# A hybrid attention/mLSTM layer: a tenth projection pair by seven products, the last gate multiplied in on chip, and the output projection's sums and loads held in order

## The chip, the cores and the metric

One core of a Trainium2 chip runs the whole layer in one launch. The metric is the device time in microseconds (us) of that core. The engines are TensorE (PE for its matmuls, PEld for its weight loads), VectorE (DVE), ScalarE (ACT), GpSimd (POOL) and SyncE (SP). DMAs are issued from two queues: SP's for most transfers, POOL's for the operands of the last stage. An engine takes its instructions in the order that was fixed when the program was built.

## The reference, cut to what matters

```python
hn = rmsnorm(x, norm_w)
proj = hn @ w_in            # q, k, v, g of 8 attention heads; qk, v, o, z, gates of 4 mLSTM heads
att = neighbourhood_attention(q, k, v, na_rpb) * silu(na_g)
h = rmsnorm(bidirectional_mlstm(silu(conv(qk)), mv, gates), head_norm_w)
mem = h * sigmoid(ml_o) * silu(ml_z)
y = rmsnorm(x + concat(att, mem) @ w_out)
```

x has 1280 tokens (1024 of a prompt and 256 of a sample) of 2048 channels in float32; concat(att, mem) has 2048 channels, 1024 of each.

## The kernel before, in words

Each float32 operand is split into a high part and a remainder (`split`, L163: ACT casts the high part, DVE subtracts it from the source), and a product is three matmuls: high by high, high by low, low by high.

**Input projection.** The output channels are taken in 128-wide columns numbered 0 to 55 (q from 0, k from 8, g from 16, qk from 24, o from 40, z from 48) and always in pairs: "pair 14" is columns 14 and 15, the k of heads 6 and 7. The first 768 tokens go first, by `pair_a` (L468). The other 512 come later, a pair in one of two ways:

- `proj_pair` (L650) multiplies directly: 4 weight pieces of 512 KB, 96 matmuls of 512 columns (L662; the trace calls them pc), 8 splits.
- `pair_s` (L1342) forms the four 256x256-blocked products from seven (Strassen's way): 7 pieces of 512 KB, 14 splits, 168 matmuls of 256 columns (L1379; their banks carry the pair's number, as S22b). Four of the seven weight operands are sums that `pair_a` of the same pair has formed already on POOL; for each pair in the list SECOND it also stores these, 16 DMAs of 128 KB (L525), into sD. `finish_s` of a pair runs between the products of the next one.

The nine pairs in SECOND go through `pair_s` one after the other (L1450). The rest go through `proj_pair` while attention runs: they are filler for TensorE. The program's order comes from a scheduler that plays the whole program on a modelled timeline; attention and mLSTM units have priority (`run`, L1304), and what is written after them fills the holes.

**Attention and mLSTM.** Head h of attention loads its q and k (2 MB, L844 and L845, into one buffer, nap{h}qk) when they have been projected and the buffer is free. The eight pairs of o and z columns are taken last of all (`late_gate`, L695, called at L1477 for 0, 2, 4, 6). For its two z columns it forms z_ = (tanh(o/2)+1) * (tanh(z/2)+1) * z, loads the mLSTM result of the same channels from mixT in DRAM (into th, named lt), multiplies with the head-norm weight w4, and stores it back into mixT (L705 to L707).

**Output projection.** With attention finished its pool is closed, and the pool mp takes its place. POOL then issues the 32 loads of the mixed operands (`mix_block`, L1490, tiles mb, 320 KB each): Ad and Ac are the mLSTM half for tokens 0 to 639 and 640 to 1279, Aa and Ae the attention half. The output has 2 halves of columns (p = 0, 1), each again by seven products (`product`, L1607), in the order 2, 5, 1, 6, 7, 4, 3 for p = 0 and 5, 1, 6, 7, 4, 3, 2 for p = 1. A product has 8 steps kk of 5 token tiles x 3 matmuls of 512 columns (L1613): 120 matmuls. `operands` (L1528) makes the operands of a step: weights straight from DRAM by `w_pure` (two steps in one 512 KB piece: wr_wp in one of the two buffers "wraw" that the input projection uses too, wp in the single buffer "wr2" of mp), or as a difference of blocks loaded by `w_block` (256 KB, wb, in one of six buffers "po", which also hold the outputs pco of `proj_pair` and lt), and for some products sums of mb tiles, all on DVE. T2 (T in the trace) is a running weight difference; its tiles, the residual tiles y (`y_init`, L1564) and fnb (the final norm's weight, L1652) lie where the projected x was, so their loads wait for the last late gate's matmuls on that x. Splits go into four buffers each for mo (mixed operand) and wo (weight).

In these names po2, or wr_wp_2_6, carries the product and the step: product 2, step 6.

Of the kernel before, what the change touches and what calls it, by code (L numbers as in the profile page):

```python
# [11 lines left out]
ALU = mybir.AluOpType  # L12
# [26 lines left out]
    GT0, QK0 + 8, GT0 + 2, QK0, KT0, GT0 + 4, KT0 + 2, GT0 + 6, KT0 + 4,  # L39
)  # L40
# [5 lines left out]
def kernel(  # L46
# [116 lines left out]
    def split(hi, lo, src, scale=None):  # L163
        if scale is None:
            S.copy(hi, src)  # L165
            V.tensor_tensor(lo, src, f(hi), op=ALU.subtract)  # L166
        else:
            S.mul(hi, src, scale)
            V.scalar_tensor_tensor(lo, src, scale, f(hi), op0=ALU.mult, op1=ALU.subtract)
# [525 lines left out]
    def late_gate(ch, X):  # L695
        os_ = proj_pair(OT0 + ch, X, True)
        for o_ in os_:
            S.activation(o_, o_, AF.Tanh, scale=0.5)
        for j, z_ in enumerate(proj_pair(ZT0 + ch, X, True)):
            k = 8 + ch + j  # L700
            th = po(f"lt{k}")[:, :GB]
            S.activation(th, z_, AF.Tanh, scale=0.5)
            V.scalar_tensor_tensor(z_, th, 1.0, z_, op0=ALU.add, op1=ALU.mult)
            V.scalar_tensor_tensor(z_, os_[j], 1.0, z_, op0=ALU.add, op1=ALU.mult)
            DM.dma_start(th, mixT[k][:, GA:])  # L705
            V.scalar_tensor_tensor(z_, th, w4_sb[:, k - 8 : k - 7], z_, op0=ALU.mult, op1=ALU.mult)
            DM.dma_start(mixT[k][:, GA:], z_)  # L707

# [768 lines left out]
    for ch in LATE:  # L1477
        late_gate(ch, X)
# [18 lines left out]
    Ac = [mix_block(1, 1, kk) for kk in range(8)]  # L1497
    Aa = [mix_block(0, 0, kk) for kk in range(8)]
# [5 lines left out]
    pair_of = {}  # L1504

    def w_block(kh, nb, kk, name):
        raw = po(f"wb_{name}")[:, :512]
        DM.dma_start(raw, w_o[nb, :, (8 * kh + kk) * 512 : (8 * kh + kk + 1) * 512])
        return raw

    def w_pure(kh, nb, kk, name):
        k = 8 * kh + kk
        if kk % 2 == 0:
            src = w_o[nb, :, k * 512 : (k + 2) * 512]
            pair_of["n"] = pair_of.get("n", -1) + 1
            if pair_of["n"] % 3 == 2:
                pair_of["w"] = mp.tile([P, 1024], F32, tag="wr2", name=f"wp_{name}")
                DM.dma_start(pair_of["w"], src)
            else:
                pair_of["w"] = w_piece(src, f"wp_{name}")  # L1520
        return pair_of["w"][:, (kk % 2) * 512 : (kk % 2 + 1) * 512]
# [82 lines left out]

    HOLD = 2

    def product(p, i, bk, first, each):  # L1607
        held = []
        tail = (p, i) == (1, 2)
# [9 lines left out]
        for kk in range(8):  # L1619
            nm = f"{p}_{i}_{kk}"  # L1620
            ms, wsrc = operands(p, i, kk)
# [13 lines left out]
            split(*w, wsrc)  # L1635
# [15 lines left out]
    for i in range(4):  # L1651
        DM.dma_start(fnb[i], fnw[i * 512 : (i + 1) * 512].partition_broadcast(P))  # L1652
    SUB = ALU.subtract
    for p in range(2):
# [27 lines left out]
        product(p, 1, ch, True, reads(ch, (0, ALU.add), done=0 if p == 0 else None))  # L1682
        y_init(p, 2)
# [96 lines left out]
```

## Time and profile before

| what | value |
|---|---|
| time of 3 runs | 2558.35, 2562.34 (median), 2562.83 us |
| the profiled execution's own time | 2565.18 us |
| its span, first to last instruction | 2563.3 us |
| granted TensorE clock, mean | 0.997 |
| PE busy, PEld busy | 2534.0 us (99%), 2368.6 us (92%) |
| DVE, ACT, POOL busy | 1972.6, 1345.0, 615.3 us |

Where the stages lie in the span, by the trace: the first projection to 1097 us, the nine pairs of SECOND from about 1173 to 1350 us, attention with its fillers to 2113 us, the rest of the late gates to 2160 us, the output projection to 2554 us. A row of the timeline has its start, its length, engine, line, operation, tiles and count, and in brackets the idle time before it and what ended that. "SPq" rows are DMA issues on SP's queue. In a row of the table by stretches, each engine's busy time is followed by its number of instructions; then come the granted clock, the busy share of the DMA engines and GB/s.

### The profile page before, as it was taken

The numbers are of one execution on the slowest core, as the hardware profiler recorded it, in microseconds if no ns is written. First come the engines' busy times: TensorE is split into PE (matmuls) and PEld (weight loads), VectorE is DVE, ScalarE is ACT, GpSimd is POOL, SyncE is SP. The second block draws the span as 40 slices with busy tenths as digits, with TensorE's granted clock in tenths as the row PEclk, the third lists the DMA queues.
The fourth block names the chain that finished last, engine by engine and source line by source line (L and its number), as shares of the span: only waits on it lengthen the run. The fifth ranks groups of instructions, "written<-read, shape, count | busy, mean of one in ns | idle before, by whom it ended". The sixth has DMA issues, their size and how long they took to land.

```text
span 2563.3 us, 44540 instructions
## 1 busy us (share of the span) xinstructions
PE 2534.0 (99%) x15054; PEld 2368.6 (92%) x15054; DVE 1972.6 (77%) x4029; ACT 1345.0 (52%) x3041; POOL 615.3 (24%) x909
## 2 busy tenths in 40 slices
PE   8999999999999999999999999999999999999998
PEld 8999999999999999999999999998988887788886
DVE  8769888888869798898875866765855665879695
ACT  8535545444444444465655666655745543344444
POOL 0535555444544444410001110100100104000001
PEclk9999999999999999999999999999999999999999
DMA  6546464536434342467768878877867849636237
GB/s 215 174 143 200 143 199 130 179 124 200 125 112 126 101 141 89 154 228 223 239 223 299 297 243 272 293 234 261 286 197 251 277 126 377 202 125 218 85 87 254
DMA packets 303483, 503.03 MB, mean 196 GB/s; under 512 B 48752, under 2 KB 191256, under 8 KB 303256
## 3 DMA queue, kind: packets, MB, share of 16 engines
q1 hardware_dynamic: 299096, 484.46, 58.9%
q0 software_dynamic: 4160, 15.73, 1.6%
q8 instruction: 119, 1.95, 0.3%
q14 instruction: 108, 0.88, 0.1%
HBM read 373.13 MB, written 126.95 MB: 195 GB/s over the span
## 4 chain that ended last, share of the span: by engine, by line
PE 92%; DMA 5%; DVE 2%; issue 1%; ACT 1%; SPq 0%; POOL 0%; ACTq 0%; POOLq 0%; DVEq 0%
PE pc L662 16%; PE po L1613 14%; PE pv L740 5%; PE fb L274 2%; PE A24b L274 1%; PE A12b L274 1%; PE A16b L274 1%; PE A44b L274 1%; PE A48b L274 1%; PE A52b L274 1%; PE A40b L274 1%; PE A20b L274 1%; PE A8b L274 1%; PE A50b L274 1%; PE A42b L274 1%; PE A22b L274 1%
## 5 line engine op out<-in xcount | busy, mean ns | idle before, releaser
L1613 PE MATMUL po<-wo,mo 128*128 128x512 f32 x1620 | 376.9, 393 | 3.7 <-ACT wo L165 2.8
L1613 PEld LDWEIGHTS po<-wo,mo 128*128 128x128 f32 x1620 | 303.6, 188 | 76.2 <-ACT wo L165 4.2
L166 DVE TENSOR_TENSOR ws<-wr,ws 128x512 fp32r<-128x512 f32 x152 | 104.3, 696 | 53.2 <-ACT ws L165 52.4
L165 ACT CAST ws<-wr 128x512 fp32r<-128x512 f32 x152 | 92.5, 617 | 70.1 <-PE pc L662 57.5
L165 ACT CAST mo<-mb 128x640 fp32r<-128x640 f32 x72 | 51.8, 726 | 92.5 <-PE po L1613 73.7
L116 POOL TENSOR_SCALAR rs<-rs 128x1 f32<-128x1 f32 x10 | 3.4, 341 | 351.2 <-DVE rs L1593 351.1
L166 DVE TENSOR_TENSOR mo<-mb,mo 128x640 fp32r<-128x640 f32 x72 | 59.1, 827 | 27.1 <-ACT mo L165 27.0
L1562 DVE TENSOR_TENSOR y<-y,po 128x512 f32<-128x512 f32 x90 | 58.5, 687 | 11.3 <-PE po L1613 11.0
L165 ACT CAST mo<-ms 128x640 fp32r<-128x640 f32 x40 | 28.9, 726 | 61.1 <-PE po L1613 32.1
L166 DVE TENSOR_TENSOR wsv<-wr_v,wsv 128x512 fp32r<-128x512 f32 x64 | 44.4, 700 | 14.2 <-ACT wsv L165 13.9
L165 ACT CAST wsv<-wr_v 128x512 fp32r<-128x512 f32 x64 | 39.0, 617 | 26.8 <-PE pv L740 15.5
L1576 ACT ACTIVATE jk<-y 128x512 f32<-128x512 f32 x40 | 25.2, 631 | 36.5 <-DVE y L1562 36.2
L413 DVE SCALAR_TENSOR_TENSOR pcv<-pco,cw_sb,pcv 128x516 f32<-128x516 f32 x48 | 36.7, 764 | 7.1 <-ACT pcv L407 7.0
L166 DVE TENSOR_TENSOR mo<-ms,mo 128x640 fp32r<-128x640 f32 x40 | 32.8, 823 | 7.6 <-ACT mo L165 7.6
L129 ACT ACTIVATE xq<-xq 128x1024 f32<-128x1024 f32 x20 | 21.2, 1061 | 31.7 <-DMA xq<-in_xtok_dram 29.2
L1081 POOL MEMSET mls_0v<- 128x2 f32 x4 | 0.4, 102 | 145.1 <-DVE S_dt.float L166 119.7
L274 PE MATMUL fb<-xg,fw 128*128 128x384 f32 x192 | 34.6, 334 | 0.0
L251 DVE TENSOR_TENSOR pco<-pc,rstdb 128x512 f32<-128x512 f32 x30 | 20.6, 687 | 17.8 <-PE pc L662 17.1
L274 PEld LDWEIGHTS fb<-xg,fw 128*128 128x128 f32 x192 | 33.4, 188 | 0.0
L778 DVE CUSTOM_DVE_ANT_0 nap_0st<-nap_0s,nap_0bt 128x384 f32<-128x384 f32 x32 | 17.7, 555 | 20.1 <-PE nap_0s L773 8.7
L1525 DVE TENSOR_TENSOR ms<-mb,mb 128x640 f32<-128x640 f32 x40 | 32.8, 823 | 0.0
L1492 POOL DMA_DIRECT2D mb<-mx x32 | 17.7, 554 | 58.8 <-DVE ws L166 24.8
(2655 smaller groups left out, 8512.4 us busy)
## 6 DMA issues: line engine op xcount, KB each, us to landing
wr<-in_w_in_dram SPq DMA_DIRECT2D x76, 512.0 KB, 4.7
wr_v<-in_w_in_dram SPq DMA_DIRECT2D x32, 512.0 KB, 5.0
wb<-in_w_o_dram SPq DMA_DIRECT2D x48, 256.0 KB, 3.0
xq<-in_xtok_dram SPq DMA_DIRECT2D x20, 512.0 KB, 4.2
mb<-mx POOLq DMA_DIRECT2D x32, 320.0 KB, 8.2
wr_wp<-in_w_o_dram SPq DMA_DIRECT2D x16, 512.0 KB, 4.0
vS<-vo SPq DMA_DIRECT2D x24, 256.0 KB, 5.1
nap_0bt<-in_rpb_tab_dram SPq DMA_DIRECT2D x32, 192.0 KB, 4.3
```

The lines of the kernel that those rows point to most:

```text
L129: S.activation(raw, raw, AF.Square, accum_out=ssq[g][:, t, q : q + 1])
L165: S.copy(hi, src)
L166: V.tensor_tensor(lo, src, f(hi), op=ALU.subtract)
L251: V.tensor_tensor(o, src, rb, op=ALU.mult)
L274: PE.matmul(o, w(a_), x(b_), start=first and m == 0, stop=last and m == 2)
L413: V.scalar_tensor_tensor(dst[:, a:n], src[:, a + j - pad : n + j - pad], cw_sb[:, ct, j : j + 1], dst[:, a:n], op0=ALU.mult, op1=ALU.add,)
L662: PE.matmul(pb[j], t[j][:, wi, c : c + P], xs[xi], start=first and m == 0, stop=last and m == 2,)
L740: PE.matmul(outs[tt], xs[:, tt * P : (tt + 1) * P], t[:, wi, q * w : (q + 1) * w], start=first and m == 0 and (gates or tt % 2 == 0), stop ...
L1525: V.tensor_tensor(t, x, y_, op=op)
L1562: V.tensor_tensor(Y[p, q, tt], Y[p, q, tt], bk, op=op)
L1576: S.activation(jk, Y[p, q, tt], AF.Square, accum_out=ss[t][:, c : c + 1])
L1613: PE.matmul(bk[tt], m[xi][:, tt * P : (tt + 1) * P], w[wi], start=first and kk == 0 and j == 0, stop=last and j == 2, skip_group_check=True,)
```

## The change

1. Pair 14 (KT0 + 6, the k of heads 6 and 7) joins SECOND: `pair_a` stores its four sums, `pair_s` takes it as the tenth, and it is no filler any more.
2. For the last late gate (ch = 6, channels 14 and 15) the load, multiplication and store through mixT are left out; z_ is kept, and multiplied into the last 512 tokens of the tiles Ac[6] and Ac[7] once these are loaded.
3. Loads: the first of every three `w_pure` pieces takes the buffer wr2, before it was the third. The residual tiles y of p = 0 other than q = 0 go to SP's queue instead of POOL's. The loads of y and fnb are traced inside a product, at step `when`, and queued on SP behind the last `w_block` load traced until then.
4. Sums: each DVE instruction that `operands` issues for step kk is placed behind the previous product's split of its step kk. This and the queueing in 3 fix a place in an engine's order; they add no wait.

```diff
 SECOND = (
     GT0, QK0 + 8, GT0 + 2, QK0, KT0, GT0 + 4, KT0 + 2, GT0 + 6, KT0 + 4,
+    KT0 + 6,
 )
...
     def late_gate(ch, X):
+        held = []
...
             V.scalar_tensor_tensor(z_, os_[j], 1.0, z_, op0=ALU.add, op1=ALU.mult)
+            held.append(z_)
+            if ch == LATE[-1]:
+                continue
             DM.dma_start(th, mixT[k][:, GA:])
...
+    for j, z_ in enumerate(last_gates):
+        k = LATE[-1] + j
+        t = Ac[k][:, GA - TH :]
+        V.scalar_tensor_tensor(t, t, w4_sb[:, k : k + 1], z_, op0=ALU.mult, op1=ALU.mult)
...
-            if pair_of["n"] % 3 == 2:
+            if pair_of["n"] % 3 == 0:
...
-            q_ = DM if p else G
+            q_ = DM if p or q else G
...
+    def scales(p):
+        for i in range(4 if p == 0 else 0):
+            DM.dma_start(fnb[i], fnw[i * 512 : (i + 1) * 512].partition_broadcast(P))
...
-            ms, wsrc = operands(p, i, kk)
+            if loads is not None and kk == when:
+                with tc.issue_after(last_load["ins"]) if kk else ExitStack():
+                    loads()
+            with tc.issue_after(done[kk]) if done else ExitStack():
+                ms, wsrc = operands(p, i, kk)
...
-            split(*w, wsrc)
+            now.append(split(*w, wsrc).ins)
...
+        done[:] = now
...
-        y_init(p, 1)
-        y_init(p, 3)
-        product(p, 5, bk, True, reads(bk, (1, ALU.add), (3, ALU.add)))
+        product(
+            p, 5, bk, True, reads(bk, (1, ALU.add), (3, ALU.add)),
+            lambda: (y_init(p, 1), y_init(p, 3)), 0 if p else 5,
+        )
...
-        product(p, 1, ch, True, reads(ch, (0, ALU.add), done=0 if p == 0 else None))
-        y_init(p, 2)
+        product(
+            p, 1, ch, True, reads(ch, (0, ALU.add), done=0 if p == 0 else None),
+            lambda: (scales(p), y_init(p, 2)), 3,
+        )
```

What moves, at three places. Up to the end of pair 6 TensorE's order is the same in both, but for the 168 matmuls of the tenth pair. First place: TensorE at the end of pair 6 (q of heads 6 and 7), the last direct pair ahead of the late gates, of before:

```order
L662 MATMUL pc6_1_19031<-x1_15h_13111,ws_6_31_19133 128x512 x2
L662 MATMUL pc6_1_19031<-x1_15l_13112,ws_6_31_19133 128x512
L662 MATMUL pc14_0_19184<-x1_0l_12804,ws_14_00_19188 128x512
L662 MATMUL pc14_0_19184<-x1_0h_12803,ws_14_00_19188 128x512 x2
L662 MATMUL pc14_0_19184<-x1_1l_12813,ws_14_00_19188 128x512
L662 MATMUL pc14_0_19184<-x1_1h_12812,ws_14_00_19188 128x512 x2
```

and of the changed kernel at the same place:

```order
L663 MATMUL pc6_1_19307<-x1_15h_13131,ws_6_31_19409 128x512 x2
L663 MATMUL pc6_1_19307<-x1_15l_13132,ws_6_31_19409 128x512
L663 MATMUL pc40_0_25388<-x1_0l_12824,ws_40_00_25392 128x512
L663 MATMUL pc40_0_25388<-x1_0h_12823,ws_40_00_25392 128x512 x2
L663 MATMUL pc40_0_25388<-x1_1l_12833,ws_40_00_25392 128x512
L663 MATMUL pc40_0_25388<-x1_1h_12832,ws_40_00_25392 128x512 x2
```

The whole pair 14, 96 matmuls in a row, has gone from here, and the first late gate (pair 40) follows at once. From the end of pair 6 to head 6's first scores stand 147 matmuls now, most of them pair 40; before, 132 stood between the end of pair 14 and these scores. After the last matmul of attention 183 matmuls of late gates are left, where there were 200.

Second place: SP's queue as the output projection begins, where the weights of product 2 are loaded, of before:

```order
L633 DMA wr_wp_2_2_26553<-in_w_o_dram 128x1024
L1537 DMA T_0_5_6_26879<-in_w_o_dram 128x512
L1537 DMA T_0_5_7_26891<-in_w_o_dram 128x512
L1652 DMA fnb_26476<-in_fnw_dram 128x512
L1652 DMA fnb_26477<-in_fnw_dram 128x512
L1652 DMA fnb_26478<-in_fnw_dram 128x512
L1652 DMA fnb_26479<-in_fnw_dram 128x512
L633 DMA wr_wp_2_6_26641<-in_w_o_dram 128x1024
L705 DMA lt_26384<-mx_149 128x512
L1508 DMA wb_5_0_26715<-in_w_o_dram 128x512
L705 DMA lt_26391<-mx_150 128x512
```

and of the changed kernel:

```order
L634 DMA wr_wp_2_2_26671<-in_w_o_dram 128x1024
L1549 DMA T_0_5_0_26815<-in_w_o_dram 128x512
L1549 DMA T_0_5_1_26842<-in_w_o_dram 128x512
L1549 DMA T_0_5_2_26869<-in_w_o_dram 128x512
L1549 DMA T_0_5_3_26896<-in_w_o_dram 128x512
L634 DMA wr_wp_2_4_26715<-in_w_o_dram 128x1024
L1549 DMA T_0_5_4_26923<-in_w_o_dram 128x512
L1549 DMA T_0_5_5_26970<-in_w_o_dram 128x512
L1549 DMA T_0_5_6_26997<-in_w_o_dram 128x512
L1549 DMA T_0_5_7_27009<-in_w_o_dram 128x512
L1530 DMA wp_2_6_26759<-in_w_o_dram 128x1024
L634 DMA wr_wp_1_0_27067<-in_w_o_dram 128x1024
```

The piece of steps 2 and 3 stood behind six T loads and stands ahead of all eight now; the piece of steps 6 and 7 stood behind fnb and stands behind T alone. fnb has moved behind the third wb load of product 1, the ten loads of y for q = 1 and 3 to between wb_5_4 and wb_5_5, and the two lt loads of the last gate and their stores are gone. On POOL the 32 mb loads stand in one row, and only 5 loads of y follow them, where 20 stood before.

Third place: DVE in product 2, of before (L706 is the last gate's multiplication, pco54 its z_, L1541 and L1538 the sums for product 5):

```order
L166 TENSOR_TENSOR mo0_2_6_26643<-mb106_26424,mo0_2_6_26643 128x640
L166 TENSOR_TENSOR wo_0_2_6_26646<-wr_wp_0_2_6_26641,wo_0_2_6_26646 128x512
L166 TENSOR_TENSOR mo0_2_7_26649<-mb107_26426,mo0_2_7_26649 128x640
L706 SCALAR_TENSOR_TENSOR pco54_0_26380<-lt14_26384,w4_sb_963,pco54_0_26380 128x512
L166 TENSOR_TENSOR wo_0_2_7_26652<-wr_wp_0_2_6_26641,wo_0_2_7_26652 128x512
L1538 TENSOR_TENSOR T2_0_5_0_26717<-T2_0_5_0_26717,wb_0_5_0_26715 128x512
L706 SCALAR_TENSOR_TENSOR pco54_1_26382<-lt15_26391,w4_sb_963,pco54_1_26382 128x512
```

and of the changed kernel (L1507 is that multiplication now, into Ac[6] and Ac[7], named mb116 and mb117):

```order
L1507 SCALAR_TENSOR_TENSOR mb117_26578<-mb117_26578,w4_sb_967,pco54_1_26508 128x512
L167 TENSOR_TENSOR mo0_2_6_26761<-mb106_26544,mo0_2_6_26761 128x640
L167 TENSOR_TENSOR wo_0_2_6_26764<-wp_0_2_6_26759,wo_0_2_6_26764 128x512
L1553 TENSOR_TENSOR mb016_26560<-mb016_26560,mb116_26576 128x640
L167 TENSOR_TENSOR mo0_2_7_26767<-mb107_26546,mo0_2_7_26767 128x640
L167 TENSOR_TENSOR wo_0_2_7_26770<-wp_0_2_6_26759,wo_0_2_7_26770 128x512
L1553 TENSOR_TENSOR mb017_26562<-mb017_26562,mb117_26578 128x640
L167 TENSOR_TENSOR mo0_5_0_26819<-mb010_26548,mo0_5_0_26819 128x640
```

The gate's multiplication has moved ahead of the last steps' splits, and each sum of product 5 follows the split of the same step of product 2.

More of the change, by code (lines that the diff above doesn't have):

```diff
@@ L165, in split @@
             S.copy(hi, src)
-            V.tensor_tensor(lo, src, f(hi), op=ALU.subtract)
+            return V.tensor_tensor(lo, src, f(hi), op=ALU.subtract)
         else:
             S.mul(hi, src, scale)
-            V.scalar_tensor_tensor(lo, src, scale, f(hi), op0=ALU.mult, op1=ALU.subtract)
+            return V.scalar_tensor_tensor(lo, src, scale, f(hi), op0=ALU.mult, op1=ALU.subtract)
     def split_a(hi, lo, src):
@@ L707, in late_gate @@
             DM.dma_start(mixT[k][:, GA:], z_)
+        return held
     def proj_v(u, X):
@@ L1477 @@
     for ch in LATE:
-        late_gate(ch, X)
+        last_gates = late_gate(ch, X)
     att_ctx.close()
@@ L1502 @@
     ss = [mp.tile([P, 4], F32, tag=f"oss{t}", name=f"oss{t}") for t in range(2 * NT)]
-    pair_of = {}
+    pair_of, last_load = {}, {}
     def w_block(kh, nb, kk, name):
         raw = po(f"wb_{name}")[:, :512]
-        DM.dma_start(raw, w_o[nb, :, (8 * kh + kk) * 512 : (8 * kh + kk + 1) * 512])
+        last_load["ins"] = DM.dma_start(
+            raw, w_o[nb, :, (8 * kh + kk) * 512 : (8 * kh + kk + 1) * 512]
+        ).ins
         return raw
@@ L1603, in finish, with product @@
             DM.dma_start(y[t * P : (t + 1) * P, i * 512 : (i + 1) * 512], out[i])
+    def scales(p):
+        for i in range(4 if p == 0 else 0):
+            DM.dma_start(fnb[i], fnw[i * 512 : (i + 1) * 512].partition_broadcast(P))
     HOLD = 2
-    def product(p, i, bk, first, each):
+    done = []
+    def product(p, i, bk, first, each, loads=None, when=0):
         held = []
+        now = []
         tail = (p, i) == (1, 2)
@@ L1649, in p_banks @@
         return [bank("pr" if next(slots) == "p" else "a", f"po{p}_{j}_{i}") for i in range(NT)]
-    for i in range(4):
-        DM.dma_start(fnb[i], fnw[i * 512 : (i + 1) * 512].partition_broadcast(P))
     SUB = ALU.subtract
```

## The prediction

> **What bounds the kernel now.** I read the page's first part, then its chain, then the table by stretches. The busy row and the chain's shares:
>
> ```profile
> PE 2534.0 (99%) x15054; PEld 2368.6 (92%) x15054; DVE 1972.6 (77%) x4029; ACT 1345.0 (52%) x3041; POOL 615.3 (24%) x909
> PE 92%; DMA 5%; DVE 2%; issue 1%; ACT 1%; SPq 0%; POOL 0%; ACTq 0%; POOLq 0%; DVEq 0%
> ```
>
> TensorE is the bound almost everywhere, so time comes from fewer TensorE microseconds or from its few gaps. The table by stretches (tenth-pair stage, pair 14, rest of attention, late gates, start and rest of the output projection) shows where gaps are:
>
> ```profile
> 1200.00:1340.00 140.00, 140.00 (x1221) 140.00 (x1220) 110.91 (x194) 83.00 (x157) 0.26 (x4) 1.00 0.73 232
> 1900.00:2113.00 213.00, 213.00 (x1170) 184.09 (x1169) 128.03 (x339) 113.13 (x271) 15.29 (x44) 1.00 0.66 213
> 2119.00:2160.00 41.00, 41.00 (x179) 33.19 (x177) 20.43 (x30) 12.32 (x21) 18.92 (x36) 1.00 1.02 397
> 2160.00:2201.00 41.00, 37.29 (x157) 28.77 (x155) 27.68 (x42) 12.61 (x21) 8.73 (x16) 1.00 0.89 325
> 2201.00:2520.00 319.00, 318.96 (x1379) 258.77 (x1380) 268.34 (x412) 144.68 (x264) 8.48 (x10) 1.00 0.46 145
> ```
>
> Only 2160 to 2201 us has gaps: 41.00 - 37.29 = 3.7 us, at the start of the output projection, at a granted clock of 1.00. TensorE's rows there, and the chain's row behind them:
>
> ```profile
> 2160.00 7.10 PE L1613 MATMUL po<-wo,mo 128*128 128x512 f32 x30
> 2168.93 15.68 PE L1613 MATMUL po<-wo,mo 128*128 128x512 f32 x65 [1.83 <-ACT wo L165]
> 2185.08 12.99 PE L1613 MATMUL po<-wo,mo 128*128 128x512 f32 x55 [0.47 <-DVE wo L166]
> 2199.01 1.65 PE L1613 MATMUL po<-wo,mo 128*128 128x512 f32 x6 [0.94 <-ACT wo L165]
> 2201.03 352.87 PE po L1613 x1524
> ```
>
> From 2201 on a matmul takes 352.87 / 1524 = 0.2315 us. The 30 + 65 + 55 + 6 = 156 before should take 36.1 us and took 2201.03 - 2160.00 = 41.0: **4.9 us are lost at this join**, waiting for split weights. Behind them stand late loads:
>
> ```profile
> 2153.34 12.37 DMA T<-in_w_o_dram
> 2165.76 15.80 DMA wr_wp<-in_w_o_dram
> 2153.86 1.47 SPq L633 DMA_DIRECT2D wr_wp<-in_w_o_dram  x1
> 2168.26 1.14 ACT L165 CAST wo<-wr_wp 128x512 fp32r<-128x512 f32 x2 [0.40 <-DMA wr_wp<-in_w_o_dram]
> DMA packets 8182, 25.19 MB, mean 394 GB/s; under 512 B 1258, under 2 KB 1258, under 8 KB 8177
> q0 software_dynamic: 4000, 15.08, 60.9%
> q1 hardware_dynamic: 4177, 10.05, 41.3%
> mb<-mx POOLq DMA_DIRECT2D x29, 320.0 KB, 8.2
> y<-in_xtok_dram POOLq DMA_DIRECT2D x20, 256.0 KB, 7.7
> fnb<-in_fnw_dram SPq DMA_DIRECT2D x4, 256.0 KB, 15.1
> ```
>
> The piece of steps 2 and 3 left at 2153.86 and was split at 2168.26 (14.4 us); the one of steps 6 and 7 left at 2165.76 and took 15.8 us. The last six rows are the DMA view of 2119 to 2183 us: 394 GB/s with all engines full, 15.08 MB from POOL's queue and 10.05 MB from SP's.
>
> **Part 1, pair 14.** The chain has the direct filler at 1892 us (158 matmuls, which hold all of pair 14) and the seven-product pairs 22 and 12, of which each starts with the same form:
>
> ```profile
> 1892.00 36.60 PE pc L662 x158
> 1311.31 2.84 PE S22bx L1379 x24
> 1330.60 2.84 PE S12bx L1379 x24
> ```
>
> Removed: 96 matmuls x 36.60 / 158 = 0.2316 us = 22.24 us. Added: one period of the seven-product stage, 1330.60 - 1311.31 = 19.29 us for 168 matmuls (0.1148 us each). Net **-2.95 us**. The period holds the splits, loads and sums of a pair already: in 1200 to 1340 us TensorE has no gap beside DVE at 110.91 of 140 us and the DMA engines at 0.73, so the 14 splits and 7 loads lie beside it. The 16 stores of 128 KB that `pair_a` adds wait on SP for POOL's sums, and the next weight load stands behind them. Two stretches of the same work, the first with two storing pairs (8 and 10), the second with one (12) and pair 14 that doesn't store:
>
> ```profile
> 211.48 9.36 PE A8b L274 x54
> 271.21 29.13 PE A26b L274 x168
> 329.46 9.49 PE A12b L274 x54
> 389.38 29.13 PE A28b L274 x168
> ```
>
> 59.73 and 59.92 us: a storing pair isn't longer. I take 0; by these rows the ends are 0.2 us either way.
>
> A rule speaks against this part. The Trainium skill, page "TensorE: Matmul & The Clock Gate", section "Back-to-back issue gap", gives a sustained spacing of about 131 ns for 512 columns and 81 ns for 128. By it (an estimate, 98 ns put in between for 256) 12.6 us would be removed and 16.4 added. The rows above disagree, 231.6 and 114.8 ns, and the measurement decides.
>
> **Part 2, attention without that filler.** Head 6 waits for pair 6 only, where it waited for pair 14. Between the end of pair 6 and head 6's scores 147 matmuls stand: almost the whole of pair 40 (22 us) and some fifty narrow ones at about 0.115 us, 28 us in all. In that time q must be stored and 2 MB loaded. What it took before:
>
> ```profile
> 1902.03 0.57 SPq L799 DMA_DIRECT2D nas6qk<-qS  x1
> 1929.90 0.61 SPq L845 DMA_DIRECT2D nap6qk<-kS  x1
> L773 PE MATMUL nap_0s<-nap6qk x12: 336/337/342, 1940.9 to 1980.1; 128*128 128x384 f32 x12
> ```
>
> Pair 6 ended at about 1893.9 (8 matmuls into the filler row), and the sample's load, behind all its stores, left 8.1 us later. Head 6's own load then has one more weight piece ahead of it on SP, whose buffer is free half-way through pair 40 (11 to 14 us, an estimate from that pair's 22), and it lands 11.0 us after it leaves (1940.9 - 1929.9, TensorE without a gap): 25 us against 28. I take 0; the stretch 1900 to 2113 shows no gap. What comes before stands in an order that doesn't change. At most the whole 81 matmuls (18.8 us) of cover lost there come back as waiting; a gain is excluded, as there is no gap to close.
>
> **Part 3, the join.** Ahead of the last piece's landing at 2181.6 stood bytes that product 2 doesn't need: 4 loads of fnb and 15 of the 20 of y, of 0.262 MB each: 5.0 MB, 12.6 us at 394 GB/s. They go behind it. Against that, the window between attention's end, which frees mp's memory, and product 2 shrinks by 17 matmuls, 3.9 us. So the last piece lands at about 2181.6 - 12.6 + 3.9 = 2172.9 in the old count, and is wanted at 2160 + 90 x 0.2315 = 2180.8 less 1.3 us for its split: 6.6 us to spare. The piece of steps 2 and 3 now leaves when its buffer is free, as the first piece did before,
>
> ```profile
> 2144.86 0.33 SPq L633 DMA_DIRECT2D wr_wp<-in_w_o_dram  x1
> 2123.04 0.33 SPq L633 DMA_DIRECT2D wr<-in_w_in_dram  x1
> 2137.66 0.40 PE L662 MATMUL pc<-x_0l,ws 128*128 128x512 f32 x1
> 2183.67 0.75 DVE L706 SCALAR_TENSOR_TENSOR pco<-lt,w_sb,pco 128x512 f32<-128x512 f32 x1
> 2186.29 0.73 DVE mo L166
> 2187.62 0.60 DVE T L1538
> 2118.01 4.00 POOL L1492 DMA_DIRECT2D mb<-mx  x7 [24.76 <-DVE ws L166]
> 2151.61 0.55 POOL L1492 DMA_DIRECT2D mb<-mx  x1 [1.07 <-DMA mb<-mx]
> ```
>
> at 2144.86; with the worst 14.4 us and the 3.9 us it is there at 2163.2, wanted at 2166.9 - 1.3 = 2165.6: 2.4 us to spare, the least of all. The piece of steps 4 and 5 leaves a quarter of a pair (5.6 us) later and is wanted 30 matmuls (6.9 us) later. The last late gate's first piece stood at 2123.04 and was wanted at 2137.66; it now stands behind two stores of the gate before it, a few microseconds out of those 14.6. The last gate's two multiplications stay on DVE (0.75 us each); Ac[6] and Ac[7] are the 23rd and 24th load on POOL; at its pace (30 from 2118.0 to 2151.6) and 3.9 us later they leave by 2149 and land by 2157, before z_ is formed from the last late gate's matmuls (2160), so no wait is added; behind it on DVE stand the splits of steps 5 to 7, which TensorE wants 17 us later. Held sums: the heaviest step on DVE is the last product of p = 0, with 8 x (0.60 + 0.73) for the sums of the next, as much for the splits, and 10 x 0.60 at the banks: 27.3 us beside 120 x 0.2315 = 27.8 of TensorE. That is tight, but splits run four steps ahead, and the long stretch after 2201 has DVE at 268.34 of 319; I take 0.
>
> So the join gives between **+3.9** (all pieces as late as before, and the shorter window on top) and **-4.9 us**; by the spare times above it is near the second, and I take -4.4, half a microsecond left for the pace. A rule stands beside this: the Trainium skill, page "DMA: Bandwidth & Descriptors", section "Issuing engines are not separate DMA queues", says that transfers of all issuers interleave on the same 16 engines, so that y on SP's queue instead of POOL's gains nothing by itself. The full window with both queues in it agrees; the 12.6 us above come from the later place alone.
>
> **The end.** After the last matmul the chain has only the last tile's sums and stores, unchanged.
>
> **Sum.** -2.95 - 4.4 + 0.4 for small waits in the reshuffled last third of attention, which the row without a gap can't exclude, = -7.0 us: span 2563.3 to 2556.3, the profiled execution's own time (1.9 us more than its span) 2565.2 to 2558.2. The profiled one lies 2.8 us over the median of the runs; on the median, 2562.34 - 7.0 = **2555.3 us**. About 0.2% (5.1 us) is what a measurement of this kernel can tell from no change.
>
> **Rivals.**
> (a) **The join keeps its wait.** The places in the queues are only an order; if the full DMA engines, with 3.9 us less lead, still bring a piece late, only pair 14's saving is left: 2562.3 - 3 = 2559.4 us. For it: 394 GB/s without a hole for 64 us, and only 2.4 us to spare at the tightest piece. Against: the 12.6 us of bytes moved out of the way.
> (b) **Slower: attention doesn't close up.** If head 6 can't start earlier, attention ends where it ended, later by the tenth pair: +19.3, less 3.9 for the shorter rest of late gates and 4.4 at the join: +11 us, 2573 us. For it: the load stands behind two weight pieces on SP. Against: 25 us against 28. Each microsecond over 3 late costs one; from 10 late it is slower than before.
> (c) **Pair 14 saves nothing**, since its 168 weight loads weigh more than the rows say: in 1200 to 1340 us PEld is busy for all of the 140.00 us, in 1900 to 2113 for 184.09 of 213. With 19.29 put up to 22.24 only the join is left: -4.0 us, 2558.3 us. Against it: the measured period holds these loads already. The spacing of the Trainium skill's page "TensorE: Matmul & The Clock Gate" points this way, and the traced paces bear it out nowhere.
>
> **Chances.** Forecast (-5.1 to -8.5 us) 0.64; (a) and mixed cases with part of the join 0.27; (b) 0.08; (c) 0.01. Faster by over 0.2%: 0.65 (the forecast and a little of a); within 0.2%: 0.27; slower: 0.08. Range: down to all of the join and the lower runs' 2 us, 2552; up to (a) with the scatter of the runs, 2561.5. Beyond lie (b) and a few extremes.
>
> **What would show it.** Pair 14: ten pairs at 19.3 us, none longer, and no filler of 96 in a row between pair 6 and pair 40; wrong if a gap opens before nap6qk's scores. Join: no wait of TensorE's L1631 on ACT or DVE wo over 0.5 us in the first 41 us, wp and wr_wp landing in time, and 0.2315 us a matmul from the first. Held sums: no gap later. What would make it wrong: waits for wr in the last late gate, or a join that moves into product 5, when wb_5 or Ac come late.

## The result, and the profile after

The changed kernel takes **2553.11 us** (median of 6 runs, 2551.69 to 2559.79); the kernel before took 2562.28 us beside it (6 runs, 2558.35 to 2562.83). The ratio is 0.9968, 95% interval 0.9958 to 0.9978. The medians lie 9.2 us apart and the ratio makes it 8.2 us, where 7.0 were forecast; the measured median lies inside the stated range of 2552 to 2561.5 us. The profiled execution took 2552.67 us with a span of 2551.0 us, at a mean granted clock of 0.999.

First the busy row on the page of the changed kernel, to lay beside that of before.

```profile
PE 2528.7 (99%) x15126; PEld 2367.7 (93%) x15126; DVE 1977.4 (78%) x4040; ACT 1347.7 (53%) x3051; POOL 605.9 (24%) x894
```

TensorE runs 72 matmuls more than before (96 wide ones out, 168 narrow ones in) and is busy 5.3 us less. The table by stretches of the changed kernel (rest of attention, late gates, start and rest of the output projection):

```profile
1900.00:2110.00 210.00, 210.00 (x1170) 182.15 (x1169) 131.16 (x355) 116.41 (x284) 13.79 (x44) 1.00 0.66 212
2110.70:2153.20 42.50, 42.50 (x184) 34.38 (x184) 19.18 (x30) 13.06 (x21) 18.91 (x35) 1.00 0.99 379
2153.20:2194.20 41.00, 41.00 (x179) 33.23 (x178) 34.69 (x54) 15.52 (x25) 1.58 (x3) 1.00 0.99 350
2194.20:2512.00 317.80, 317.80 (x1377) 258.04 (x1376) 265.65 (x408) 143.44 (x261) 9.36 (x10) 1.00 0.46 145
```

No gap is left from 1900 us to the end. The first 41 us of the output projection held 3.7 us of gaps before and hold none now, although the DMA engines are fuller than before (0.99 in the third row, 0.89 in the same 41 us before). TensorE's chain of the changed kernel at the places that the prediction named:

```profile
1332.59 2.84 PE S12bx L1385 x24
1351.88 2.84 PE S14bx L1385 x24
...
1907.33 18.10 PE pc L663 x78
...
2110.66 42.57 PE pc L663 x183
2153.23 388.53 PE po L1631 x1680
```

From pair 12 to pair 14 it is 19.29 us; the longest filler row left is of 78 matmuls, where one of 158 stood that held pair 14; and all 1680 matmuls of the output projection stand in one piece, 388.53 / 1680 = 0.2313 us each. Before, the projection took 393.5 us from its first matmul to its last (2160.0 to 2553.5; the same count, from the start of the first matmul to the start of the last, gives 388.3 now).

Where the 12.3 us between the two spans lie, from TensorE's rows: until the first of the ten (nine) pairs +2.0 (1173.3, now 1175.3); from there to the projection's first matmul -8.9 (986.7, now 977.8), of which -2.95 are pair 14's and the other 6 are waits and slow stretches in heads 2 to 4; the projection -5.2; the tail -0.2.

### The profile page after: what moved, and what is told of

It reads as the page before. It is cut to its first block, busy times and chain, and to the rows that moved or that the text cites. A ratio compares the mean times of both kernels' runs of the same rounds, so it can differ in the third digit from the quotient of the medians.

```text
span 2551.0 us, 44749 instructions
## 1 busy us (share of the span) xinstructions
PE 2528.7 (99%) x15126; PEld 2367.7 (93%) x15126; DVE 1977.4 (78%) x4040; ACT 1347.7 (53%) x3051; POOL 605.9 (24%) x894
## 4 chain that ended last, share of the span: by engine, by line
PE 83%; DMA 2%; DVE 1%; ACT 0%; SPq 0%; issue 0%; ACTq 0%; POOLq 0%; POOL 0%; DVEq 0%
PE pc L663 15%; PE po L1631 15%; PE pv L746 5%; PE A16b L275 1%; PE A52b L275 1%; PE A48b L275 1%; PE A44b L275 1%; PE A40b L275 1%; PE A20b L275 1%; PE A50b L275 1%; PE A42b L275 1%; PE A18b L275 1%; PE A54b L275 1%; PE A70b L275 1%; PE A68b L275 1%; PE A36b L275 1%
## 5 line engine op out<-in xcount | busy, mean ns | idle before, releaser
L167 DVE TENSOR_TENSOR ws<-wr,ws 128x512 fp32r<-128x512 f32 x144 | 98.0, 690 | 39.3 <-ACT ws L166 37.1
L784 DVE CUSTOM_DVE_ANT_0 nap_0st<-nap_0s,nap_0bt 128x384 f32<-128x384 f32 x32 | 17.7, 553 | 20.3 <-PE nap_0s L779 7.9
L787 ACT ACTIVATE nap_0st<-nap_0st,nap_0sm 128x384 f32<-128x384 f32 x32 | 19.7, 617 | 22.1 <-DVE nap_0sm L784 22.1
```

Source lines behind the costliest of these rows:

```text
L167: return V.tensor_tensor(lo, src, f(hi), op=ALU.subtract)
L787: S.activation(st, st, AF.Exp, bias=sm[:, 0:1], scale=-1.0, accum_out=sm[:, 2:3])
```

## The experiments

Twelve kernels ran, in three groups, each group beside runs of the kernel before. Since executions of one kernel lie up to 10 us apart (e1_pair14: 2560.57 to 2570.83), the finer measure is the projection's length in the trace, "po length" below, from the start of its first matmul to the start of its last: 388.2 to 388.3 us is the floor without a gap. It comes from one execution of each kernel. "Heads" is the time from the first of the seven-product pairs to the projection. Each ratio is to the kernel before in the same group, whose medians were 2561.64, 2561.49 and 2561.17 us in the three groups; the rows "before" and "after" are those of the result.

| kernel | pairs | gate on chip | new loads | held sums | median, us | ratio to before (95%) | heads, us | po length, us |
|---|---|---|---|---|---|---|---|---|
| before | 9 | | | | 2562.28 | | 986.7 | 393.5 |
| e0_before | 9 | | | | 2562.47 | 1.0004 (0.9995 to 1.0012) | 983.0 | 393.7 |
| e7_dram | 9 | | | | 2560.89 | 0.9998 (0.9989 to 1.0007) | 981.8 | 393.4 |
| e3_gate | 9 | x | | | 2561.98 | 1.0003 (0.9994 to 1.0012) | 982.2 | 394.7 |
| e11_loads | 9 | | x | | 2556.86 | 0.9983 (0.9974 to 0.9991) | 978.6 | 390.0 |
| e2_join | 9 | x | x | x | 2555.80 | 0.9980 (0.9971 to 0.9989) | 982.9 | 388.2 |
| e1_pair14 | 10 | | | | 2563.24 | 1.0011 (1.0002 to 1.0019) | 982.4 | 400.1 |
| e9_pair_hold | 10 | | | x | 2557.81 | 0.9991 (0.9982 to 1.0000) | 978.2 | 394.5 |
| e8_pair_gate | 10 | x | | | 2555.81 | 0.9980 (0.9971 to 0.9989) | 977.1 | 390.7 |
| e10_pair_loads | 10 | | x | | 2553.84 | 0.9973 (0.9964 to 0.9983) | 979.3 | 390.7 |
| e5_no_hold | 10 | x | x | | 2554.37 | 0.9971 (0.9959 to 0.9982) | 977.3 | 390.1 |
| e6_no_loads | 10 | x | | x | 2552.83 | 0.9965 (0.9952 to 0.9977) | 978.2 | 388.9 |
| e4_no_gate | 10 | | x | x | 2551.13 | 0.9958 (0.9946 to 0.9971) | 977.6 | 388.2 |
| after | 10 | x | x | x | 2553.11 | 0.9968 (0.9958 to 0.9978) | 977.8 | 388.3 |

### First group: do the parts add, and what are the 6 us in heads 2 to 4?

Two theories. A: pair 14 and the join add up, and the 6 us in attention are scatter from one execution to the next. B: the change takes waits out of attention, by its new order or by where things lie in DRAM.

**e0_before** is the kernel before, unchanged.

> The kernel before, run once more. In the profile of the change, 6 us of its gain stand in attention's heads 1 to 4, whose order on TensorE did not change: the waits of 0.5, 2.5 and 1.9 us for the q and k of heads 2, 3 and 4 and slices at a granted clock of 0.97 are not there. Theory A (scatter): these waits come and go from execution to execution of one kernel; the profile of this run shows heads 2 to 4 with other waits than before (each anywhere from 0 to 3 us), and its runs scatter over some 5 us. Theory B (the change does it): they stand here again within 0.5 us, at a granted clock of 0.997.

**e7_dram** adds four unused tensors in DRAM, as many as pair 14's sums take:

```diff
+    for i in SUMS:
+        dram.tile([P, 1024], F32, tag=f"sD14_{i}", name=f"sD14_{i}")
```

> The kernel before, with four more scratch tensors of 512 KB declared in DRAM where pair 14's sums would lie, which nothing uses. No instruction changes. Theory A: same time within 0.1%, waits of heads 2 to 4 by chance. Theory B by way of memory places (what lies where in DRAM changes how fast the 2 MB loads land): the waits of heads 2 to 4 go, -6 us.

TensorE's waits for q and k of heads 2 to 4, first of the kernel before as first profiled, then of e0_before, the same kernel (columns: total, times, longest):

```profile
PE nap_0s L773 <- DMA nap3qk<-kS: 2.5, 1, 2.5
PE nap_0s L773 <- DMA nap4qk<-kS: 1.9, 1, 1.9
PE nap_0s L773 <- DMA nap2qk<-kS: 0.5, 1, 0.5
```

```profile
PE nap_0s L773 <- DMA nap3qk<-kS: 1.7, 1, 1.7
...
PE nap_0s L773 <- DMA nap2qk<-kS: 0.4, 1, 0.4
PE nap_0s L773 <- DMA nap4qk<-kS: 0.4, 1, 0.4
```

The same program waited 4.9 us in one execution and 2.5 in the other, and its heads took 986.7 and 983.0 us. The profile of before also has two stretches at a granted clock of 0.50, right behind its waits for heads 3 and 4; together they lost 3.4 us, and neither e0_before nor the changed kernel has one there. Placement in DRAM does nothing that the runs can tell (e7_dram, 0.9998, 0.9989 to 1.0007). So the 6 us are mostly the draw of one profile, and B falls as the account of them. In medians of runs the gain is 9.2 us, not 12.3.

**e1_pair14** is before with the tenth pair alone, **e2_join** is the changed kernel without it:

```diff
     GT0, QK0 + 8, GT0 + 2, QK0, KT0, GT0 + 4, KT0 + 2, GT0 + 6, KT0 + 4,
+    KT0 + 6,
```

> Only pair 14 by seven products. Theory A: -3.0 us (22.24 us of filler removed, 19.29 added), with waits in heads 2 to 4 that follow no edit, and the join still losing 4 to 5 us. Theory B: -3 and -6 in heads 1 to 4, together about -9 us, so that the edit takes away the waits for q and k.

> Everything but pair 14: last gate on chip, loads and sums held in order. The matmuls of the output projection should go without a gap, 388.5 us for 1680 instead of 393.9: -5.4 us at the join. Theory A: -5.4 us in all, with waits in heads 2 to 4 by chance. Theory B: -5.4 us, and the waits for q and k of heads 2 to 4 (4.9 us) stand as before.

The join alone gave 5.8 us (2561.64 in its group to 2555.80), and from there the tenth pair gave 2.7 more (3.3 when each is taken against the kernel before of its own group). But the tenth pair alone gave nothing: it was slower by 0.1%. The parts don't add. (The profiled execution of e1_pair14, 2570.83 us, is the slowest of its 11; its median is 1.6 us over that of before in its group, which with -2.95 for the pair leaves +4.6 for the projection, 398 rather than the 400.1 of the trace, an estimate.) TensorE's rows at the start of the projection in e1_pair14:

```profile
2159.14 27.95 PE L1614 MATMUL po<-wo,mo 128*128 128x512 f32 x120
2187.59 0.73 PE L1614 MATMUL po<-wo,mo 128*128 128x512 f32 x2 [0.50 <-ACT wo L166]
2190.07 8.30 PE L1614 MATMUL po<-wo,mo 128*128 128x512 f32 x28 [1.75 <-DVE wo L167]
2202.21 137.43 PE L1614 MATMUL po<-wo,mo 128*128 128x512 f32 x582 [3.84 <-ACT wo L166]
```

The whole first product is without a gap, in spite of the shorter lead, and the join breaks one product later. SP's queue in e1_pair14 shows why the first product is in time, and the chain what broke behind it:

```profile
2144.79 0.33 SPq L634 DMA_DIRECT2D wr_wp<-in_w_o_dram  x1
2146.57 2.19 SPq L1538 DMA_DIRECT2D T<-in_w_o_dram  x4
2149.58 0.33 SPq L634 DMA_DIRECT2D wr_wp<-in_w_o_dram  x1
2152.15 2.78 SPq L1538 DMA_DIRECT2D T<-in_w_o_dram  x4
2156.71 0.33 SPq L634 DMA_DIRECT2D wr_wp<-in_w_o_dram  x1
2158.86 6.95 SPq L1653 DMA_DIRECT2D fnb<-in_fnw_dram  x4
2167.35 2.21 SPq L706 DMA_DIRECT2D lt<-mx  x2
```

```profile
2153.54 15.63 DMA T<-in_w_o_dram
...
2169.23 14.94 DMA lt<-mx
...
2184.20 0.04 DVE pco L707
```

With ten pairs the scheduler lays the queue anew: the last piece of product 2 leaves ahead of the four fnb and 2.4 us before the projection's first matmul, where it left 5.8 us after it before. That is not the change to the loads; one more entry in a list did it. What it didn't move is the load of the last gate, lt, which leaves behind fnb and lands at 2184.17. VectorE stands in its order at L707 for it, with the sums of product 5 behind, and TensorE waits for their splits.

### Second group: leave one part out

Theories now: **gate** (what holds the join back is VectorE's stand for the last gate) against **loads** (it is the bytes queued ahead of product 2's pieces), and whether the hold is worth anything.

**e3_gate**, before with the last gate multiplied in on chip:

```diff
+            held.append(z_)
+            if ch == LATE[-1]:
+                continue
...
+    for j, z_ in enumerate(last_gates):
+        k = LATE[-1] + j
+        t = Ac[k][:, GA - TH :]
+        V.scalar_tensor_tensor(t, t, w4_sb[:, k : k + 1], z_, op0=ALU.mult, op1=ALU.mult)
```

> Before plus one part: the last gate is multiplied in on chip (no store and load again of the two last gate tiles). Nine pairs, the old order of loads, sums not held. The output projection took 393.5 us before, 388.3 without a gap (after, and join without the tenth pair), 400.1 with the tenth pair alone, where VectorE stood until 2184 for the load of the last gate and TensorE for VectorE. Gate theory (the round trip of the last gate holds VectorE, and with it the weights of the first products): the projection comes to 388.3 to 390 and the time to 3 to 5 us below before. Loads theory (the weight pieces of product 2 come late because bytes not yet wanted are queued ahead of them): the projection stays at 392 to 394 and the time within 1.5 us of before. Both: somewhere between, 390 to 392.

**e4_no_gate**, the changed kernel without these lines:

```diff
-            if ch == LATE[-1]:
-                continue
...
-    for j, z_ in enumerate(last_gates):
-        k = LATE[-1] + j
-        t = Ac[k][:, GA - TH :]
-        V.scalar_tensor_tensor(t, t, w4_sb[:, k : k + 1], z_, op0=ALU.mult, op1=ALU.mult)
```

> After, with the last gate again stored and loaded (all else as after: ten pairs, the new order of loads, held sums). Gate theory: VectorE stands for the load of the last gate as in the tenth pair alone, a wait of some us on the weights of the products after the first comes back, the projection takes 394 to 400 and the time is 4 to 10 us above after (2557 to 2563). Loads theory: with the scales and inputs no longer ahead of it the load lands some us earlier than 2184 and nothing waits; projection 388 to 389.5, time within 1.5 us of after.

**e5_no_hold**, the changed kernel without the hold of the sums (part 4 of the change):

```diff
-            with tc.issue_after(done[kk]) if done else ExitStack():
-                ms, wsrc = operands(p, i, kk)
+            ms, wsrc = operands(p, i, kk)
```

> After, without holding the sums of the product before behind the weights of the product after (the order of VectorE's instructions is the scheduler's again). If the hold is worth nothing, as the prediction has it (VectorE 27.3 us of work beside 27.8 of TensorE in a product): projection 388.3 within 0.5, time within 1 us of after. If the hold carries part of the gain: a wait of TensorE on the low halves (VectorE L167) of 0.5 to 3 us in the first products, projection 389 to 392, time 1 to 4 us above after.

**e6_no_loads**, the changed kernel with the old loads:

```diff
-            if pair_of["n"] % 3 == 0:
+            if pair_of["n"] % 3 == 2:
...
-            q_ = DM if p or q else G
+            q_ = DM if p else G
...
-            if loads is not None and kk == when:
-                with tc.issue_after(last_load["ins"]) if kk else ExitStack():
-                    loads()
...
+    scales(0)
...
+        y_init(p, 1)
+        y_init(p, 3)
...
+        y_init(p, 2)
```

> After, with the old loads of the projection: scales and first inputs early in the queue, the wide weight pieces at the old place of the three, inputs of one group on GpSimd's queue. Ten pairs, gate on chip, held sums stay. Gate theory: VectorE no longer stands for a load, so only the old wait of product 2 is left with 3.9 us less lead: projection 390 to 394, time 1 to 5 us above after. Loads theory: the pieces of product 2 land as late as in the tenth pair alone or later, and the projection takes 396 to 400, the time 7 to 11 us above after.

On nine pairs the gate alone gave nothing: the last piece still leaves behind fnb. SP's queue in e3_gate, and TensorE's rows there:

```profile
2151.43 1.38 SPq L633 DMA_DIRECT2D wr_wp<-in_w_o_dram  x1
...
2156.82 5.01 SPq L1661 DMA_DIRECT2D fnb<-in_fnw_dram  x4
2163.55 0.33 SPq L633 DMA_DIRECT2D wr_wp<-in_w_o_dram  x1
```

```profile
2157.56 7.10 PE L1622 MATMUL po<-wo,mo 128*128 128x512 f32 x30
2166.68 15.51 PE L1622 MATMUL po<-wo,mo 128*128 128x512 f32 x65 [2.02 <-ACT wo L165]
2182.99 40.79 PE L1622 MATMUL po<-wo,mo 128*128 128x512 f32 x175 [0.80 <-DVE wo L166]
```

The last one leaves at 2163.55, 6.0 us into the projection, and the 2.02 us gap is the 1.83 of before. Its 394.7 us lie above the range of either theory: waits of 1.18 and 0.97 us stand further on, 67 and 176 us into the projection, which before doesn't have. With ten pairs, either the gate or the new loads can be left out: without the gate the projection takes 388.2 us, without the loads 388.9. Both the gate theory (for e4_no_gate) and the loads theory (for e6_no_loads) fall; e4_no_gate came out 2.0 us below the changed kernel's median, where the loads theory had allowed 1.5. In e4_no_gate the lt loads stand ahead of fnb and y, the multiplication on VectorE is in time, and the chain is one piece. SP's row and the chain's row in e4_no_gate:

```profile
2156.07 0.93 SPq L708 DMA_DIRECT2D lt<-mx  x2
```

```profile
2152.03 388.46 PE po L1625 x1680
```

Without the hold the projection took 390.1 us, with one wait for a low half that the changed kernel doesn't have. It stands 162 us into the projection, in the sixth product and not in the first ones, where it was expected. TensorE's row of e5_no_hold, and the chain that leads to it:

```profile
2312.99 209.30 PE L1631 MATMUL po<-wo,mo 128*128 128x512 f32 x903 [1.30 <-DVE wo L167]
```

```profile
2305.61 5.93 DMA wb<-in_w_o_dram
2311.64 0.60 DVE T L1550
2312.24 0.70 DVE wo L167
```

VectorE isn't full here: it is busy for 16.52 of the 22 us ahead of 2312 (for 17.57 of the same 22 us in the changed kernel). It stands 3.22 us for a load of wb, which a sum of T needs, and the split that TensorE waits for comes behind that sum. So the wait is one of order, of the same kind as the stand for lt.

### Third group: a theory of three waits

(1) With nine pairs product 2's pieces leave too late; ten pairs or the new loads move them ahead. (2) With the old loads lt lands too late, and VectorE stands for it; the gate on chip or the new loads take that away. (3) Without the hold, sums stand ahead of splits in VectorE's order, and a product further on waits. The rival is that the hold alone decides, since every kernel with it was at most at 388.9 us until then.

**e8_pair_gate** is e1_pair14 and e3_gate together, **e9_pair_hold** the tenth pair with the hold of e5_no_hold's diff, **e10_pair_loads** the tenth pair with the loads of e6_no_loads' diff, **e11_loads** those loads alone. The diff of e11_loads against before, in its core:

```diff
-            if pair_of["n"] % 3 == 2:
+            if pair_of["n"] % 3 == 0:
...
-            q_ = DM if p else G
+            q_ = DM if p or q else G
...
+            if loads is not None and kk == when:
+                with tc.issue_after(last_load["ins"]) if kk else ExitStack():
+                    loads()
...
-    for i in range(4):
-        DM.dma_start(fnb[i], fnw[i * 512 : (i + 1) * 512].partition_broadcast(P))
```

> Before plus the tenth pair and the last gate on chip; old loads, sums not held. Theory of three waits: (1) product 2's last weight piece stands behind the four loads of scales with nine pairs, but ahead of them with ten, where the scheduler places them anew; (2) with the old loads VectorE stands for the load of the last gate, which the gate on chip takes away; (3) without the hold VectorE's sums push the low halves of some later product back by 1 to 2 us. So here (1) and (2) are away and (3) is left: the projection takes 389.5 to 391 us, the time is 6 to 9 us below before. Rival, the hold is what each good kernel so far had (388.2 to 388.9 us with it, 390.1 to 400.1 without): then the projection takes 393 to 400 and the time is 0 to 4 us below before.

> Before plus the tenth pair and the held sums; old loads, last gate stored and loaded. Theory of three waits: (1) is away by the tenth pair, (2) stays, since the load of the last gate stands behind eight loads of T, two weight pieces and four scales and lands some 30 us after TensorE has begun: the projection takes 394 to 401 us and the time is within 3 us of before. Rival, the hold alone makes the join smooth: projection 388 to 389.5, time 7 to 10 us below before.

> Before plus the tenth pair and the new order of loads; last gate stored and loaded, sums not held. Theory of three waits: the load of the last gate now stands ahead of scales and inputs, so (1) and (2) are away and (3) is left: projection 389 to 391 us, time 6 to 9 us below before. Rival (the hold is needed): projection 393 to 400, time 0 to 4 us below before.

> Before plus the new order of loads alone, nine pairs. Theory of three waits: product 2's last piece and the load of the last gate both leave ahead of the scales, so the 1.8 us wait 7 us into the projection goes, which the gate on chip alone left at 2.0; projection 388.5 to 391 us, time 3 to 5 us below before. Rival (bytes queued ahead are not what is waited for): projection 393 to 395, time within 1.5 us of before.

All four projections came out inside what the three waits expect: 390.7, 394.5, 390.7 and 390.0 us (the times of e8_pair_gate and e9_pair_hold lie 0.6 and 0.4 us outside). The rival falls with e9_pair_hold, whose chain is that of e1_pair14 again:

```profile
2146.43 15.29 DMA T<-in_w_o_dram
...
2161.78 15.23 DMA lt<-mx
...
2177.03 0.04 DVE pco L709
...
2191.30 38.79 PE po L1625 x160
```

e11_loads has one wait of 0.98 us late in the projection and none at its start. TensorE's rows there:

```profile
2155.65 169.76 PE L1624 MATMUL po<-wo,mo 128*128 128x512 f32 x732
2326.39 200.59 PE L1624 MATMUL po<-wo,mo 128*128 128x512 f32 x866 [0.98 <-DVE y L1567]
```

And in e10_pair_loads three waits of 0.35 to 0.40 us are left, the first of them 47 us into the projection; the table by stretches has VectorE busy for all of the 20 us ahead of the first of them (in e4_no_gate, which has the hold, for 16.39 of the same 20 us):

```profile
2199.94 16.20 PE L1625 MATMUL po<-wo,mo 128*128 128x512 f32 x69 [0.35 <-DVE wo L167]
2216.53 98.53 PE L1625 MATMUL po<-wo,mo 128*128 128x512 f32 x425 [0.39 <-ACT wo L166]
2315.47 209.48 PE L1625 MATMUL po<-wo,mo 128*128 128x512 f32 x903 [0.40 <-DVE wo L167]
```

```profile
2180.00:2200.00 20.00, 19.64 (x86) 15.64 (x84) 20.00 (x31) 8.88 (x14) 0.00 (x0) 1.00 0.98 348
```

What each part is worth depends on the others. The new loads: 3.5 us of projection with nine pairs (393.5 to 390.0), 9.4 with ten (400.1 to 390.7), 0.6 where gate and hold are there (388.9 to 388.3). The gate: 9.4 with ten pairs and the old loads (400.1 to 390.7), nothing once the loads are new (388.2 without, 388.3 with). The hold: 1.8 to 2.5 with ten pairs (390.1, 390.7 and 390.7 to 388.3, 388.9 and 388.2), and 5.6 where lt is late (400.1 to 394.5). Two cautions belong to this. The 400.1 us of e1_pair14 are those of the slowest of its executions, and about 5 us of them were lost to a lower granted clock (last section); by medians, each against before in its own group, the three differences from e1_pair14 are 8.9 us for the loads, 7.0 for the gate and 5.0 for the hold. And the 1.8 to 2.5 us of the hold are differences of single traces; in medians they are 2.0, 3.3 and 3.0 us. Each part keeps its sign by both measures; the sizes differ by up to 2.4 us. So the changed kernel has one part more than it needs. Whether e4_no_gate at 2551.13 us is faster than the changed kernel isn't settled: the intervals overlap, and their projections are equal.

## Why the prediction was right, point by point

- **Pair 14** (-2.95): right. The added period, from pair 12 to pair 14, is 19.29 us, and with the join in place the tenth pair is worth 2.7 us in medians (e2_join 2555.80, after 2553.11) and 3.0 (e11_loads 2556.86, e10_pair_loads 2553.84). Storing four more sums costs nothing, as taken: from pair 12 to pair 28, the stretch in which pair 14 stores now, it was 59.92 us before and is 59.74 in e1_pair14.
- **Attention** (0): right. Head 6's scores began 10.8 us after their load left (1926.75 to 1937.5, where before it was 11.0) without a wait. The 25 us that I counted from the end of pair 6 to the landing came out by luck, from two terms that were both off: the load left 17.7 us after that end (1909.0 to 1926.75) and not 14, and it landed at most 7.3 us later and not 11, since I had read the landing off the scores, which began after it. 3.4 us were to spare. "A gain is excluded, as there is no gap to close" is refuted by the pair of profiles (6 us in heads 2 to 4) and saved by the medians: the waits of 0.4 to 2.6 us for q and k come and go between executions of one program. The view that misled was mine: I read the stretch from 1900 us on and not the heads before it, where the profile before held 4.9 us of waits. Heads took 982.6 us in the median of the six profiles with nine pairs and 978.0 in the eight with ten; past pair 14's 2.95, the 1.6 us left are within that scatter, and what they are isn't settled.
- **The join** (-4.4, between +3.9 and -4.9): right in kind, and 0.8 too small. 393.5 to 388.3 is -5.2: no half microsecond was left for the pace, and my count of 4.9 stopped at 2201 us. The piece that I had called the tightest, that of steps 2 and 3 with 2.4 us to spare, was cast at 2152.56, before the projection began. The piece of steps 6 and 7 was there 12.5 us after the projection began, where I had 12.9; its cast in the changed kernel, after that of the piece of steps 4 and 5:

```profile
2157.68 0.62 ACT L166 CAST wo<-wr_wp 128x512 fp32r<-128x512 f32 x1 [0.21 <-DMA wr_wp<-in_w_o_dram]
...
2165.64 0.62 ACT L166 CAST wo<-wp 128x512 fp32r<-128x512 f32 x1 [1.22 <-DMA wp<-in_w_o_dram]
```

- **Why the join closed**: half right. "The 12.6 us above come from the later place alone" fits nine pairs, where e11_loads closes the join; but it changes the buffer, the queue of y and the place of the loads together, and no run takes these apart. In the changed kernel the tenth pair alone had brought that piece ahead of fnb already (e1_pair14), which I could have seen by asking for the order with only that edit. What the loads and the gate then share is lt, a load I had priced only where it was removed, and not as what VectorE would stand for with 3.9 us less lead.
- **Held sums** ("that is tight, but splits run four steps ahead ... I take 0"): 0 is right for the changed kernel, whose projection has no gap, but the reason given is not what makes it so. Without the hold the same work costs 1.8 to 2.5 us of projection, with VectorE full for 20 us in e10_pair_loads, and standing in its order for a load in e5_no_hold. A count of 27.3 beside 27.8 us says that the work fits into a product, not that each split stands early enough in it.
- **+0.4 for small waits**: not found; the stretch 1900 to 2110 shows TensorE busy for 210.00 of 210.00 us.
- **Rival (a)** named the right danger, the shorter lead, and the wrong place. With the tenth pair alone the saving was lost entirely (1.0011), though through product 5 and lt, not through product 2.
- **Sum**: -2.95 - 5.2 - 0.2 = -8.4 us by the terms as measured, against -9.2 in the medians, whose interval (-10.8 to -5.6 us, 0.9958 to 0.9978 of 2562.28) holds both and the forecast. The narrower band of -5.1 to -8.5 us, to which I gave 0.64, holds the 8.2 us of the ratio and not the 9.2 of the medians. That the terms could be added at all was partly luck: alone they gave +1.6 (e1_pair14) and -5.8 us (e2_join), -4.2 together, and the -9.2 come about because the loads and the gate also take away the stand for lt that the tenth pair would have brought, which the prediction didn't see.

## What to carry to other kernels

A join of two stages has several waits in a row, and the first hides the ones behind it: closing one can show up as no gain at all (e3_gate), and a shorter lead can cost more than it saved (e1_pair14). Try each edit alone and each left out before paying for all of them, and where a scheduler makes the order, look at the order of each edit alone, since a list entry far away can move the loads that matter. For an engine that works through its instructions in order, look at where each stands and which load the one ahead of it waits for, not only at the sum of the work.

## What the runs showed of the hardware

A wait of TensorE can cost more than its own length. The table by stretches of e1_pair14, from behind its first two waits on (the granted clock is the third number from the right):

```profile
2190.00:2198.00 8.00, 7.93 (x28) 6.35 (x28) 6.99 (x11) 1.51 (x3) 1.09 (x2) 0.79 0.63 223
2198.00:2202.00 4.00, 0.37 (x2) 0.00 (x0) 2.31 (x4) 1.19 (x2) 0.00 (x0) 0.89 0.00 0
2202.00:2206.00 4.00, 3.79 (x9) 3.02 (x10) 3.81 (x7) 1.99 (x4) 0.00 (x0) 0.50 0.46 136
2206.00:2210.00 4.00, 4.00 (x14) 3.14 (x14) 4.00 (x7) 1.25 (x2) 0.00 (x0) 0.76 0.69 215
```

After the wait of 3.84 us (2198.4 to 2202.2) the clock was 0.50 for four microseconds and 0.76 for four more; the 0.79 of the first row is a stretch at 0.50 as well, behind the wait of 1.75 us. The waits there are 6.3 us in all (0.50, 1.75, 3.84 and 0.17 much later), by the rows the lower clock lost 5.1 us more (8 x 0.21 + 4 x 0.11 + 4 x 0.50 + 4 x 0.24; 0.4 of it while TensorE waited anyway), and the projection is 11.8 us longer than the smooth one. The same stands in heads 2 to 4 of before, where 2.54 us of waiting for head 3 ended at 1634.38:

```profile
1632.00:1636.00 4.00, 1.62 (x10) 1.61 (x11) 1.43 (x5) 0.74 (x2) 0.57 (x1) 0.96 1.05 383
1636.00:1640.00 4.00, 4.00 (x24) 4.00 (x24) 3.18 (x10) 2.13 (x7) 1.77 (x6) 0.62 1.05 395
```

The Trainium skill, page "TensorE: Matmul & The Clock Gate", section "Why this matters for your kernels", asks for no idle gap of TensorE above about 3 us, since one idle window halves the clock. The rows agree with the drop to 0.50 after 3.84 us; they differ in that 2.54 us was enough for 0.62.

The length of a wait alone doesn't decide whether the clock drops. In these profiles each wait of 2.5 us or more between the pairs and the end of the projection was followed by a stretch at 0.50 (2.54, 2.57, 2.98 and 3.84 us). Of the shorter ones, 1.75 (e1_pair14), 1.86 (before, head 4) and 1.90 us (e2_join, head 3) were, and 1.83 (before's join), 1.99 (e1_pair14, head 2) and 2.02 us (e3_gate) were not. What makes the difference is not shown. At a full clock, too, a wait can cost a little more than its length: in e5_no_hold the clock stayed at 1.00, and a single wait of 1.30 us goes with a projection 1.8 us longer.
